# Two blocks on one core: row statistics in paused steps, a decay without mask matmuls, narrow time-step tiles, wider attention-value matmuls

## The chip, the cores and the metric

The program runs on one core of one Trainium2 chip. The metric is the device time of one execution in microseconds (us), the median over several runs. The kernel before takes 2222.25 us (three runs, 2221.23 to 2222.55). A difference below about 0.2%, 4.4 us, cannot be told from none here.

## What is computed

Two blocks follow each other on 512 rows of width 1024 (the second adds 16 meta rows: 528). All weight products are done to nearly float32 precision, each as three fp32r matmuls (high x high, high x low, low x high). The parts that the change touches:

```python
def ssd_chunked(x, dt, a_head, bm, cm):          # 32 heads, 4 groups, chunks of 128 rows
    a_cs = jnp.cumsum(a, axis=-1)                # a = dt * a_head, negative
    seg = a_cs[..., :, None] - a_cs[..., None, :]
    decay = jnp.where(causal, jnp.exp(jnp.where(causal, seg, 0.0)), 0.0)
    cb = jnp.einsum("bclgn,bcsgn->bcgls", cc, bc)
    y_diag = jnp.einsum("bcgrls,bcsgrp->bclgrp", cb[:, :, :, None] * decay, xs)
...
dt = jax.nn.softplus(dt_raw + dt_bias)           # dt_raw: 32 columns of h @ w_in
...
def layer_norm(x, g, b): ...                     # mean and variance over 1024
def rmsnorm(x, g): ...                           # mean square over 1024 or 512
...
o = jnp.einsum('bnhgqk,bnkhd->bnqhgd', p, v)     # sliding window, 8 heads of 64, 128 queries a block
```

## The kernel before

Activations are held transposed (features on partitions, rows on the free axis) as a high and a low tile. Weights stream from one DRAM array in the order in which they are used: `Weights.take` (line 99) hands out 128x128 blocks; units of eight blocks are loaded (`raw`), split on ScalarE (`whi`) and VectorE (`wlo`), and two of each are kept (`wheld` ones stay longer). `gemm` and `gemm_ab` issue three matmuls (`pm`) a block and segment; `gemm_ab` does the rows in two halves (`si` 0 and 1), all output tiles `m` of the first half, then those of the second, so that the second half's operand can still be in the making.

Work beside the gemms is written as generators. `start(gen, every)` (line 204) puts one into `tasks`; after each block `tick` (line 219) steps a task on every `every` ticks. `every=0` runs it to its end at once; `finish` (line 213) drains what is left. This sets only the order in which instructions are recorded; a list scheduler then orders each engine's queue by that order, by priorities (`tc.high_priority`) and by when it takes operands to be ready. On the chip each engine works its queue strictly in that order.

Row statistics need a sum over partitions. `colsum` (line 266) does it with `pcs` matmuls of one column, `meansq` scales on VectorE (`msv`), `rsqrt` (line 260) takes the power -1/2 on GpSimd (`rs_y`), `rstd_bcast` (line 284) spreads the result over partitions with `pbc` matmuls, and only then can VectorE scale the tiles. `pcs` and `pbc` are recorded directly one after the other, and pushed later by the priorities `LATE` and `LATE2` (40 and 60 places). `layer_norm`, `ssd_norm`, `pre_scale`, `post_pre` and `normed` all use it. In the text a place has the name of its use: sn0 to sn3 (state space groups), cn, ln1, ln2, ps (scale of the next block's input), an and yn (attention and convolution norms), post and post2 (after the mixer and the MLP); a last digit 0 or 1 is the half `si`, and ps has the layer ahead of it.

The state space part (`ssd_core`, line 595) makes for each of 32 heads a 128x512 tile `pA` = cumulated decay of the row, spread over partitions by a bf16 matmul with three-part decays, plus a mask matmul (`identb` x `mask_ssd`, -1e30 above the diagonal); four ScalarE Exp of 128 columns with bias `nacs` give `dec`, VectorE multiplies by `cbs`, and `py` matmuls use it. `time_steps` (line 506) makes dt with weights repeated four times, so that each of four 32-row strips of a 128x512 result holds all columns.

In `attention` (line 966) each unit (a block of 128 queries, two heads' pairs) multiplies the transposed probabilities `pT` with values `vt` (or `vm`, the 16 meta rows) into `po`, 64 output partitions a matmul, one head's 128 columns at a time.

Of the kernel before, what the change touches and what calls it, by code (L numbers as in the profile page):

```python
# [32 lines left out]
NV = 0  # L33
# [9 lines left out]
B_ID, B_SSD, B_ATT, B_SEL = 0, 128, 256, 512  # L43
NC16 = 512 + 32
# [71 lines left out]
def block_kernel(ctx, tc, xin, meta, wst, wdt, vec, c32, c16, out, order):  # L116
# [102 lines left out]
    def tick():  # L219
        for t in list(tasks):  # L220
            t[2] += 1
            while t[2] >= t[1]:
                t[2] -= t[1]
                if next(t[0], tasks) is tasks:
                    tasks.remove(t)
                    break
# [19 lines left out]
    identb = cb16[:, B_ID:B_ID + 128]  # L246
# [37 lines left out]
    def rstd_bcast(acc, tk, nt, width, eps):  # L284


        v = meansq(acc, tk, nt, width, eps)
        r = rsqrt(v, tk, nt)
        ps = PX("pbc")
        with tc.high_priority(offset=-LATE2):  # L290
            for j in range(nt):
                mmul(ps[:, j * tk:(j + 1) * tk], r[:, j:j + 1].to_broadcast([tk, 128]),
                     ident[:tk, :tk], start=True, stop=True)
        return ps[:, 0:nt * tk]
# [103 lines left out]
    def layer_norm(tiles, seg, cb, acc=None):  # L398

        c0, cn, tk, nt = seg  # L400
        sl = slice(c0, c0 + cn)
        if acc is None:
            acc = F("lnacc")[:, :cn]
            tt(acc, tiles[0][:, sl], tiles[1][:, sl], op=ALU.add)
            for i in range(2, 8):
                tt(acc, acc, tiles[i][:, sl], op=ALU.add)
                yield
        mu = PX("pmu")[:, :cn]
# [8 lines left out]
        r = rstd_bcast(sq.t, tk, nt, 1024, 1e-5)  # L417
# [88 lines left out]
    def time_steps():  # L506
        raw = A("wdt", F32).rearrange("p a b -> p (a b)")[:, 0:1024]
        dma(nc.scalar, raw, wdt)
        wh, wl = (A(f"wdt{j}").rearrange("p a b -> p (a b)")[:, 0:1024] for j in range(2))
        split((wh, wl), raw)  # L510
        ps = PM("pdt")
        for k in range(8):
            sl = slice(k * 128, (k + 1) * 128)
            mmul(ps, wh[:, sl], hA[k][:, 0, 0:512], start=(k == 0), stop=False)
            mmul(ps, wh[:, sl], hA[k][:, 1, 0:512], start=False, stop=False)
            mmul(ps, wl[:, sl], hA[k][:, 0, 0:512], start=False, stop=(k == 7))
# [4 lines left out]
        for c in range(4):  # L521
            q = slice(32 * c, 32 * c + 32)
            act(x[q], ps[q, c * 128:(c + 1) * 128], AF.Identity, bias=V("ssm_dt_bias")[q])
# [20 lines left out]
        dtT, nacs, dtds, cd = (tok[:, i] for i in range(4))  # L544
# [5 lines left out]
        ts(nacs, pv[:, 1], -1.0, None, op0=ALU.mult)  # L550
# [12 lines left out]
        mmul(pl[:, 0:128], ident[:, 127:128].to_broadcast([128, 128]), nacs.rearrange("p c h -> p (c h)"), start=True, stop=True)  # L563
        plv = pl[:, 0:128].rearrange("p (c h) -> p c h", c=4)
        act(cd, plv, AF.Exp, scale=-1.0)
        tt(dtds, nacs, plv, op=ALU.subtract)
        act(dtds, dtds, AF.Exp)
        tt(dtds, dtT, dtds, op=ALU.mult)
        DT["t"] = ahl, dtT, nacs, dtds, cd
# [25 lines left out]
    def ssd_core(gr):  # L595
        ahl, dtT, nacs, dtds, cd = DT["t"]
# [7 lines left out]
        acopy(cbs, pcb)  # L604
# [11 lines left out]
        for hf in range(2):  # L616
# [30 lines left out]
            for t in range(2):  # L647
# [64 lines left out]
    def ssd_norm(gr, acc, xs_):  # L712
        r = rstd_bcast(acc, 128, 4, 512, 1e-5)
# [10 lines left out]
    def conv_norm():  # L724
# [10 lines left out]
        yield from layer_norm([cts[i] for i in range(8)], (0, 512, 128, 4), cb)  # L735
# [109 lines left out]
    def ln1(si):  # L845
# [9 lines left out]
        yield from layer_norm([RS[i] for i in range(8)], x_seg(si), cb, RS["acc", si])  # L855
# [48 lines left out]
    def pre_scale(sq, si, seg, nxt):  # L904


        c0, cn, tk, nt = seg
        sq.flush()
        yield
        if nxt["square"]:  # L910
            v = meansq(sq.t, tk, nt, 1024, 1e-6)
            nxt["eps", si] = S([128, 4], "eps")[:tk, :nt]
            stt(nxt["eps", si], v, 1e-6, v, op0=ALU.mult, op1=ALU.mult)
        else:
            acopy(nxt["rb"][:, c0:c0 + cn], rstd_bcast(sq.t, tk, nt, 1024, 1e-6))

    def ln2(si):
# [11 lines left out]
        yield from layer_norm(h, (c0, cn, tk, nt), cb, RS["acc", si])  # L929
        scales.append(start(pre_scale(sq, si, seg, pre), EV['ps']))  # L930

    def post_pre(fs, sums, segs, si, gain, l, nxt, eps):
# [4 lines left out]
        r = rstd_bcast(sums[si].t, tk, nt, 1024, eps(si))  # L937
# [13 lines left out]
    def normed(ys, gain, l, seg, dst):  # L951
# [6 lines left out]
        r = rstd_bcast(sq.t, tk, nt, 512, 1e-6)  # L958
# [7 lines left out]
    def attention(l, Q, K, vt, vm, yP, norm, norms):  # L966
        def unit(b, pr):
# [58 lines left out]
            for i in range(2):  # L1026
                for j, (o, n, v) in enumerate(kbs):
                    for r in range(2):
                        mmul(po[64 * r:64 * r + 64, 128 * i:128 * i + nq], v[:n, 64 * r:64 * r + 64],
                             pTs[r][:n, (2 * j + i) * 128:(2 * j + i) * 128 + nq],  # L1030
                             start=(j == 0), stop=(j == len(kbs) - 1))
# [39 lines left out]
    for l in range(2):  # L1071
# [69 lines left out]
        for m in (0, 1, 2, 3)[WI - 2:]:  # L1141
            qkv[m] = qkv_tile(m)
            for p, (c0, cn) in zip(gemm(acts, w_in, one, m), one):
# [8 lines left out]
                              lambda si: normed(ya, "attn_out_g", l, psegs[si], yn[0:4]), norms), EV['att'])  # L1152
# [29 lines left out]
        def out_evac(m, si, ps):  # L1182
# [6 lines left out]
        post = lambda si: pend.append(start(post_pre(o, sums, psegs, si, "mix_post_g", l, pre, lambda si: 1e-6),  # L1189
                                            EV['post'] * (1 - si)))  # L1190
        gemm_ab(yn, w_out, range(8), gsegs, out_evac, lambda: post(0),
                first=(FO, 4, lambda: [run(normed(yc, "conv_out_g", l, psegs[si], yn[4:8]))
                                     for si in range(2)]))
# [47 lines left out]
        if l == 0:  # L1241
            ws.hold(16, WI)
        post = lambda si: pend.append(start(post_pre(f, fsums, psegs, si, "mlp_post_g", l, pre,
                                                     lambda si: mlp["eps", si]),
# [3 lines left out]
    while pend:  # L1248
# [10 lines left out]
SUML, LATE, LATE2 = 10, 40, 60  # L1259
# [5 lines left out]
      "ln1": 3, "ps": 4, "an": 4, "ln2": 0, "post": 5, "post2": 1.5}  # L1265

# [7 lines left out]
def _constants():  # L1274
# [15 lines left out]
    b[:, B_ID:B_ID + 128] = np.eye(128)  # L1290
    s = np.arange(128)
    m = np.where(s[:, None] <= s[None, :], 0.0, -1e30)
# [58 lines left out]
def _build():  # L1351
# [3 lines left out]
              ("wdt", (128, 1024), F32), ("vec", (128, NV), F32), ("c32", (128, NC32), F32),  # L1355
# [25 lines left out]
```

## Time and profile before

| | us |
|---|---|
| median of three runs | 2222.25 |
| the profiled execution, its own time | 2217.79 |
| its span | 2215.9 |
| TensorE busy | 2180.1 |
| VectorE busy | 1449.1 |
| ScalarE busy | 917.2 |
| GpSimd busy | 32.9 |

The page gives for each engine the time in which an instruction of its ran. A matmul's recorded duration overlaps the next one's: what a matmul costs in a stream is the distance from its start to the next start. "Idle before" is what an engine waited for before an instruction. The granted clock is TensorE's share of full speed in a stretch; it has two levels, 1.00 (2.4 GHz) and 0.50 (1.2 GHz).

### The profile page before, as it was taken

To read this page: it belongs to the slowest core of one execution; us is meant where nothing else is said; L and a number is where in the kernel's file an instruction comes from. 1 tells how busy PE (TensorE), PEld (TensorE's weight loads), DVE (VectorE), ACT (ScalarE), POOL (GpSimd) and SP (SyncE) were. 2 spreads that over 40 slices of the span, in tenths; PEclk is the share of its full clock that TensorE was granted. 3 is DMA by queue.
4 is the path that set the end of the run, shared out by engine and by line. 5 is a ranking of instruction groups with operands and counts; after the bars stand their busy time and mean duration, and the time that the engine had idled before them with its cause. 6 is when DMAs were issued, how large, how long until landed. Compare 5 with 4: busy or idle time off the path is not lost.

```text
span 2215.9 us, 33490 instructions
## 1 busy us (share of the span) xinstructions
PE 2180.1 (98%) x13786; PEld 1928.6 (87%) x13792; DVE 1449.1 (65%) x2650; ACT 917.2 (41%) x1700; POOL 32.9 (1%) x43
## 2 busy tenths in 40 slices
PE   8999999999999999999999999999999999999997
PEld 6887787878889888889999999999998899888897
DVE  7999899966668766636888653234378866423436
ACT  4344543444434444424646543224253554322323
POOL 0000000000000000000000000000000000000000
PEclk9999999999999999999999999999999999999999
DMA  4222121212232122224312212222251131222224
GB/s 154 96 81 73 58 82 71 96 59 94 95 133 77 58 95 95 95 96 172 125 58 96 77 40 95 96 90 83 96 182 58 60 131 39 96 95 95 95 96 152
DMA packets 32408, 206.86 MB, mean 93 GB/s; under 512 B 4608, under 2 KB 6912, under 8 KB 8192
## 3 DMA queue, kind: packets, MB, share of 16 engines
q1 hardware_dynamic: 30816, 203.01, 25.8%
q8 instruction: 108, 1.77, 0.3%
q10 hardware_dynamic: 1440, 1.71, 0.2%
q14 instruction: 44, 0.36, 0.1%
HBM read 202.61 MB, written 2.10 MB: 92 GB/s over the span
## 4 chain that ended last, share of the span: by engine, by line
PE 95%; DVE 1%; issue 1%; POOL 1%; DMA 0%; ACT 0%; POOLq 0%; DVEq 0%
PE pm L187 88%; PE po L187 2%; PE pbc L187 1%; PE py L187 1%; PE ppt L191 1%; POOL rs_y L263 1%; PE psc L187 1%; PE pA L187 1%; PE pcs L187 1%; PE pst L187 0%; PE ptx L191 0%; DMA raw<-wst 0%; DVE wlo L172 0%; PE pdt L187 0%; DVE bst L439 0%
## 5 line engine op out<-in xcount | busy, mean ns | idle before, releaser
L172 DVE TENSOR_TENSOR wlo<-raw,whi 128x1024 fp32r<-128x1024 f32 x335 | 409.8, 1224 | 499.9 <-ACT whi L184 498.1
L184 ACT CAST whi<-raw 128x1024 fp32r<-128x1024 f32 x335 | 351.1, 1049 | 755.3 <-PE pm L187 737.8
L187 PE MATMUL pm<-h,whi 128*128 128x512 f32 x1760 | 559.6, 397 | 0.0
L187 PE MATMUL pm<-r,whi 128*128 128x264 f32 (+2 forms) x2128 | 407.4, 302 | 0.0
L187 PEld LDWEIGHTS pm<-h,whi 128*128 128x128 f32 x1760 | 328.8, 188 | 77.0 <-issue 1.6
L187 PE MATMUL pm<-yn,whi 128*128 128x264 f32 (+2 forms) x1728 | 392.4, 330 | 0.1
L187 PE MATMUL pm<-h,wlo 128*128 128x512 f32 x880 | 349.4, 397 | 0.0
L187 PEld LDWEIGHTS pm<-r,whi 128*128 128x128 f32 x2128 | 318.5, 188 | 14.7 <-issue 0.2
L187 PEld LDWEIGHTS pm<-yn,whi 128*128 128x128 f32 x1728 | 275.6, 188 | 30.6 <-ACT yn L184 0.5
L187 PE MATMUL pm<-r,wlo 128*128 128x264 f32 (+2 forms) x1064 | 267.9, 301 | 0.1
L187 PE MATMUL pm<-yn,wlo 128*128 128x264 f32 (+2 forms) x864 | 247.2, 328 | 0.0
L187 PEld LDWEIGHTS pm<-h,wlo 128*128 128x128 f32 x880 | 165.0, 187 | 37.1 <-issue 0.9
L187 PE MATMUL pm<-ff,whi 128*128 128x264 f32 (+2 forms) x944 | 189.9, 307 | 0.0
L187 PEld LDWEIGHTS pm<-r,wlo 128*128 128x128 f32 x1064 | 178.9, 188 | 7.8 <-DVE wlo L172 0.3
L175 DVE SCALAR_TENSOR_TENSOR c<-v,vv,c 128x501 f32<-128x501 f32 (+27 forms) x240 | 167.0, 730 | 1.4 <-ACT c L181 0.9
L187 PEld LDWEIGHTS pm<-yn,wlo 128*128 128x128 f32 x864 | 147.3, 188 | 15.1
L187 PEld LDWEIGHTS pm<-ff,whi 128*128 128x128 f32 x944 | 146.4, 190 | 7.9
L187 PE MATMUL pm<-ff,wlo 128*128 128x264 f32 (+2 forms) x472 | 127.5, 306 | 0.0
L187 PE MATMUL pm<-yn,wheld 128*128 128x264 f32 (+1 forms) x960 | 125.8, 289 | 0.0
L187 PEld LDWEIGHTS pm<-yn,wheld 128*128 128x128 f32 x960 | 120.2, 192 | 0.6 <-issue 0.3
L187 PEld LDWEIGHTS pm<-ff,wlo 128*128 128x128 f32 x472 | 83.0, 190 | 4.0
L172 DVE TENSOR_TENSOR sum<-sum,sq 128x256 f32<-128x256 f32 (+2 forms) x171 | 73.2, 434 | 20.2 <-ACT sq L181 18.8
(255 smaller groups left out, 2372.9 us busy)
## 6 DMA issues: line engine op xcount, KB each, us to landing
raw<-wst SPq DMA_DIRECT2D x188, 1024.0 KB, 4.8
xr<-xin SPq DMA_DIRECT2D x4, 512.0 KB, 5.2
trig<-c SPq DMA_DIRECT2D x2, 528.0 KB, 5.7
raw<-wst SPq DMA_DIRECT2D x2, 512.0 KB, 7.5
out<-r ACTq DMA_DIRECT2D x8, 128.0 KB, 1.8
out<-r SPq DMA_DIRECT2D x8, 128.0 KB, 1.8
wdt<-wdt ACTq DMA_DIRECT2D x1, 512.0 KB, 5.3
vv<-vec SPq DMA_DIRECT2D x1, 385.0 KB, 7.8
```

The lines of the kernel that those rows point to most:

```text
L172: return first(nc.vector.tensor_tensor(o, a, b, op=op), o)
L175: return first(nc.vector.scalar_tensor_tensor(o, a, c, b, op0=op0, op1=op1), o)
L184: return first(nc.scalar.copy(o, a), o)
L187: r = first(nc.tensor.matmul(o, a, b, start=start, stop=stop), o)
L191: return first(nc.tensor.transpose(o, a, i), o)
L263: nc.gpsimd.tensor_tensor(y, v, mhalf[:p, :n], op=ALU.pow)
```

## The change

- Tasks count down to zero; a generator may yield a number, a pause of so many ticks (never less than `every`). `every=0` no longer runs a task to its end: it stops at the first pause. `colsum` and `rstd_bcast` lose their priorities; `rstd_bcast` pauses `GAP[use][0]` ticks ahead of `pcs` and `GAP[use][1]` ticks between `rs_y` and `pbc`. `finish` still drains without regard to pauses. The convolution's norms (yn) are started ahead of the output gemm.
- The 32 mask matmuls are gone. ScalarE computes `Relu(acs - pA)` (4 x 128 columns) and one more `Exp(-x)` over 512 columns; the mask (now 1 and 0) is multiplied into `cbs` once a group, on VectorE instead of a ScalarE copy.
- The time-step weights are 128x256 float32, not split and not repeated; 64 float32 matmuls of 32 output partitions x 128 columns, in four column positions, take the place of 24 fp32r matmuls of 128x512.
- `po`: where the block has 128 queries, both heads' 256 columns in one matmul (half as many).

```diff
     def start(gen, every=0):
         t = [gen, every, every / 2]
-        if every:
-            tasks.append(t)
-        else:
-            finish(t)
+        tasks.append(t)
+        if not every:
+            advance(t)
         return t
+    def advance(t):
+        while t[2] <= 0:
+            n = next(t[0], tasks)
+            if n is tasks:
+                tasks.remove(t)
+                break
+            t[2] += t[1] if n is None else max(n, t[1])
...
     def colsum(acc, tk, nt):
         ps = PX("pcs")
-        with tc.high_priority(offset=-LATE):
-            for j in range(nt):
-                mmul(ps[:tk, j:j + 1], acc[:, j * tk:(j + 1) * tk], ones[:, 0:1], start=True,
-                     stop=True)
+        for j in range(nt):
+            mmul(ps[:tk, j:j + 1], acc[:, j * tk:(j + 1) * tk], ones[:, 0:1], start=True, stop=True)
...
+        yield GAP[use][0]
         v = meansq(acc, tk, nt, width, eps)
         r = rsqrt(v, tk, nt)
+        yield GAP[use][1]
         ps = PX("pbc")
-        with tc.high_priority(offset=-LATE2):
-            for j in range(nt):
...
-        ps = PM("pdt")
+        ps = PM("pdt")[:, 0:128]
         for k in range(8):
...
+            sl = slice(k * 32, (k + 1) * 32)
+            for j in range(2):
+                for c in range(4):
+                    mmul(ps[32 * c:32 * c + 32], raw[:, sl],
+                         hA[k][:, j, c * 128:(c + 1) * 128].bitcast(F32),
+                         start=(k == 0 and j == 0), stop=(k == 7 and j == 1))
...
-        acopy(cbs, pcb)
+        tt(v3(cbs), v3(pcb), mask_ssd, op=ALU.mult)
...
                     mmul(pA, sel[:, h + r:h + r + 1].to_broadcast([128, 128]), ahl, start=True,
-                         stop=False)
-                    mmul(pA, identb, mask_ssd, start=False, stop=True)
+                         stop=True)
...
-                        act(dec[:, sl], pA[:, sl], AF.Exp, bias=nacs[:, c, h + r:h + r + 1])
+                        act(dec[:, sl], pA[:, sl], AF.Relu, scale=-1.0, bias=acs[:, c, h + r:h + r + 1])
+                    act(dec, dec, AF.Exp, scale=-1.0)
...
-            for i in range(2):
+            for i in range(1 if nq == 128 else 2):
+                cn = 256 if nq == 128 else nq
...
-                        mmul(po[64 * r:64 * r + 64, 128 * i:128 * i + nq], v[:n, 64 * r:64 * r + 64],
+                        c = (2 * j + i) * 128
+                        mmul(po[64 * r:64 * r + 64, 128 * i:128 * i + cn], v[:n, 64 * r:64 * r + 64],
...
+GAP = {"cn": (1, 3), "sn0": (1, 3), "sn1": (1, 3), "sn2": (1, 3), "sn3": (1, 3), "ln10": (2, 20), "ln11": (2, 41),
+       "ln20": (2, 36), "ln21": (2, 40), "ps00": (2, 26), "ps01": (2, 20), "ps10": (2, 20), "ps11": (2, 20), "an0": (2, 3), "an1": (2, 20), "yn0": (2, 6), "yn1": (2, 6),
+       "post0": (2, 6), "post1": (2, 12), "post20": (2, 12), "post21": (2, 28)}
```

How the change moves TensorE's queue, at three places. First a head of the state space part, before and then now (`pA` the decay tile, `cb` the mask and selector constants, `pm` the gemm that runs beside it):

```order
L187 MATMUL pm<-h_114,wlo 128x512
L187 LDWEIGHTS cb_92
L187 MATMUL pA<-ahl,cb_92 128x512
L187 LDWEIGHTS cb_92
L187 MATMUL pA<-cb_92 128x512
```

```order
L187 MATMUL pm<-h_114,wlo 128x512
L187 LDWEIGHTS cb_92
L187 MATMUL pA<-ahl,cb_92 128x512
L187 MATMUL pm<-h_115,whi 128x512 x2
```

The second `pA` matmul, the mask, is gone; the gemm follows at once.

Second, TensorE where the second block's first projection changes from half 0 to half 1 (place ln21; `ff22` to `ff29` are its eight operand tiles), before and then now:

```order
L187 MATMUL pbc_8652<-cc_91,rs_y_8650 128x128 x2
L187 MATMUL pm_8846<-ff25_6108,wheld_8788 128x264
L187 MATMUL pm_8846<-ff25_6108,wheld_8789 128x264
L187 MATMUL pm_8846<-ff26_6183,wheld_8788 128x264 x2
L187 MATMUL pm_8846<-ff26_6183,wheld_8789 128x264
L187 MATMUL pm_8846<-ff27_6258,wheld_8788 128x264 x2
L187 MATMUL pm_8846<-ff27_6258,wheld_8789 128x264
L187 MATMUL pm_8846<-ff28_6333,wheld_8788 128x264 x2
L187 MATMUL pm_8846<-ff28_6333,wheld_8789 128x264
L187 MATMUL pm_8846<-ff29_6408,wheld_8788 128x264 x2
L187 MATMUL pm_8846<-ff29_6408,wheld_8789 128x264
L187 MATMUL pm_8873<-ff22_5907,wheld_8576 128x264
```

```order
L187 MATMUL pm_8809<-ff28_6366,wheld_8751 128x264 x2
L187 MATMUL pm_8809<-ff28_6366,wheld_8752 128x264
L187 MATMUL pm_8809<-ff29_6441,wheld_8751 128x264 x2
L187 MATMUL pm_8809<-ff29_6441,wheld_8752 128x264
L187 MATMUL pbc_8836<-cc_91,rs_y_8702 128x128 x2
L187 MATMUL pm_8892<-ff22_5940,wheld_8609 128x264
L187 MATMUL pm_8918<-ff22_5940,wheld_8613 128x264
L187 MATMUL pm_8977<-ff22_5940,wheld_8648 128x264
```

Before, 14 gemm matmuls of half 0 stand between `pbc` and the first matmul of half 1 (the row `pm_8873<-ff22`); now none does.

Third, TensorE after the first layer's MLP (place post21; `r2_16` to `r2_23` are the next layer's operand tiles), before and then now:

```order
L187 MATMUL pcs_15118<-cc_91,sum_14994 88x1 x3
L187 MATMUL pm_15383<-r2_21_13589,wheld_15278 128x264
L187 MATMUL pm_15383<-r2_21_13589,wheld_15279 128x264
L187 MATMUL pm_15383<-r2_22_13654,wheld_15278 128x264 x2
L187 MATMUL pm_15383<-r2_22_13654,wheld_15279 128x264
L187 MATMUL pm_15383<-r2_23_13721,wheld_15278 128x264 x2
L187 MATMUL pm_15383<-r2_23_13721,wheld_15279 128x264
L187 MATMUL pm_15426<-r2_16_13258,wheld_15282 128x264 x2
L187 MATMUL pbc_15126<-cc_91,rs_y_15124 128x88 x3
```

```order
L187 MATMUL pcs_15188<-cc_91,sum_15043 88x1 x3
L187 MATMUL pm_15389<-r2_16_13259,wheld_15319 128x264 x2
L187 MATMUL pm_15389<-r2_16_13259,wheld_15320 128x264
L187 MATMUL pm_15389<-r2_17_13326,wheld_15319 128x264
L187 MATMUL pbc_15285<-cc_91,rs_y_15194 128x88 x3
```

Between `pcs` and `pbc` stood ten gemm matmuls, and now stand four.

## Rows read from the trace of the kernel before

**Rows 1.** The page: busy time, share of the span, instructions.

```profile
PE 2180.1 (98%) x13786; PEld 1928.6 (87%) x13792; DVE 1449.1 (65%) x2650; ACT 917.2 (41%) x1700; POOL 32.9 (1%) x43
```

**Rows 2.** Waits of TensorE: us in total, times, longest us.

```profile
PE pbc L187 <- POOL rs_y L263: 13.9, 16, 1.6
...
PE pm L187 <- ACT ff L181: 0.3, 1, 0.3
```

**Rows 3.** Chain of waits, 165 to 177 us: start, us, what.

```profile
165.51 0.45 PE pA L187 x2
165.96 4.17 PE pm L187 x18
170.12 1.02 PE py L187 x16
```

**Rows 4.** Chain of waits, whole span.

```profile
45.55 5.59 PE pdt L187 x24
...
1147.17 1.47 PE po L187 x16
...
1167.12 1.02 PE po L187 x16
```

**Rows 5.** Groups by shape: count | busy us, mean ns of one | idle before.

```profile
L181 ACT ACTIVATE dec<-pA,tok 128x128 f32<-128x128 f32 x128 | 37.2, 372 | 34.8 <-PE pA L187 33.3 <-PE py L187 1.5
L172 DVE TENSOR_TENSOR dec<-dec,cbs 128x512 f32<-128x512 f32 x32 | 21.9, 687 | 3.9 <-ACT dec L181 3.8
L181 ACT ACTIVATE fth<-cg 128x512 f32<-128x512 f32 x22 | 13.9, 632 | 46.3 <-DVE cg L175 46.3
```

**Rows 6.** GpSimd's powers: all (ns min/median/max), then six in time, us.

```profile
L263 POOL TENSOR_TENSOR rs_y<-msv,mhalf x29: 695/847/2104, 230.4 to 2205.9; 128x2 f32<-128x2 f32 x12, 88x3 f32<-88x3 f32 x12, 128x4 f32<-128x4 f32 x5
...
311.68 1.43 POOL L263 TENSOR_TENSOR rs_y<-msv,mhalf 128x4 f32<-128x4 f32 x1 [79.86 <-DVE msv L178]
...
518.30 1.01 POOL L263 TENSOR_TENSOR rs_y<-msv,mhalf 128x4 f32<-128x4 f32 x1 [108.82 <-DVE msv L178]
...
1045.10 1.61 POOL L263 TENSOR_TENSOR rs_y<-msv,mhalf 128x2 f32<-128x2 f32 x1 [336.43 <-DVE msv L178]
1067.92 1.80 POOL L263 TENSOR_TENSOR rs_y<-msv,mhalf 88x3 f32<-88x3 f32 x1 [21.21 <-DVE msv L178]
...
1218.49 0.97 POOL L263 TENSOR_TENSOR rs_y<-msv,mhalf 88x3 f32<-88x3 f32 x1 [32.01 <-DVE msv L178]
1223.98 1.05 POOL L263 TENSOR_TENSOR rs_y<-msv,mhalf 88x3 f32<-88x3 f32 x1 [4.52 <-DVE msv L178]
```

**Rows 7.** Timeline of TensorE at 1044 us (place ln20).

```profile
1044.15 0.61 PE L187 MATMUL pcs<-cc,sum 128*128 128x1 f32 x4
...
1046.76 0.71 PE L187 MATMUL pbc<-cc,rs_y 128*128 128x128 f32 x4 [1.44 <-POOL rs_y L263]
```

**Rows 8.** Timeline of TensorE at 1223 us (place yn).

```profile
1223.08 0.56 PE L187 MATMUL pcs<-cc,sum 128*88 128x1 f32 x6
1225.09 0.54 PE L187 MATMUL pbc<-cc,rs_y 88*128 88x88 f32 x2 [1.45 <-POOL rs_y L263]
```

**Rows 9.** Chain of waits, 1080 to 1092 us (place ln21).

```profile
1079.92 3.29 PE pm L187 x27
...
1085.48 0.43 DVE r L172
...
1085.93 1.09 ACT r L181 x2
1087.03 0.41 ACT ff L181
```

**Rows 10.** Stretches: us, PE, PEld, DVE, ACT, POOL busy, granted clock, DMA share, GB/s.

```profile
1047.80:1051.20 3.40, 3.40 (x19) 3.40 (x18) 2.12 (x7) 2.13 (x4) 0.00 (x0) 0.50 0.67 275
...
1225.30:1232.10 6.80, 6.55 (x32) 6.32 (x32) 4.86 (x13) 3.16 (x8) 0.85 (x1) 0.50 0.01 4
...
1802.10:1805.60 3.50, 3.38 (x16) 3.39 (x17) 3.50 (x11) 2.50 (x6) 0.06 (x1) 0.51 0.02 5
```

More of the change, by code (lines that the diff above doesn't have):

```diff
@@ L220, in tick @@
         for t in list(tasks):
[L221 to L226, printed above, removed]
+            t[2] -= 1
+            advance(t)
     cc = const.tile([128, C_COS], F32, tag="cc", name="cc")
@@ L396, in block_kernel, with layer_norm @@
     ALL = [(0, 512)]
-    def layer_norm(tiles, seg, cb, acc=None):
+    def layer_norm(tiles, seg, cb, use, acc=None):
         c0, cn, tk, nt = seg
@@ L407, in layer_norm @@
                 yield
+        yield GAP[use][0]
         mu = PX("pmu")[:, :cn]
@@ L416, in layer_norm @@
         sq.flush()
-        r = rstd_bcast(sq.t, tk, nt, 1024, 1e-5)
+        r = yield from rstd_bcast(sq.t, tk, nt, 1024, 1e-5, use)
         for i in range(8):
@@ L520, in time_steps @@
         x, e, u, s = w("dtx"), w("dte"), w("dtu"), w("dts")
[L521 to L523 removed]
+        act(x, ps, AF.Identity, bias=V("ssm_dt_bias"))
         stt(e, x, -1.0, x, op0=ALU.mult, op1=ALU.max)
@@ L543, in time_steps @@
         tok = const.tile([128, 4, 4, 32], F32, tag="tok", name="tok")
-        dtT, nacs, dtds, cd = (tok[:, i] for i in range(4))
+        dtT, acs, dtds, cd = (tok[:, i] for i in range(4))
         pt = PX("pdt2")
@@ L595, in ssd_core @@
     def ssd_core(gr):
-        ahl, dtT, nacs, dtds, cd = DT["t"]
+        ahl, dtT, acs, dtds, cd = DT["t"]
         bc, xs_ = XG[gr]
@@ L733, in cb @@
             del cts[i]
-        yield from layer_norm([cts[i] for i in range(8)], (0, 512, 128, 4), cb)
+        yield from layer_norm([cts[i] for i in range(8)], (0, 512, 128, 4), cb, "cn")
     gate = {}
@@ L853, in cb @@
             tt(lo, x, hi.bitcast(F32), op=ALU.subtract)
-        yield from layer_norm([RS[i] for i in range(8)], x_seg(si), cb, RS["acc", si])
+        yield from layer_norm([RS[i] for i in range(8)], x_seg(si), cb, f"ln1{si}", RS["acc", si])
     ws.hold(8, 6)
@@ L910, in pre_scale @@
         if nxt["square"]:
+            yield GAP["ps00"][0]
             v = meansq(sq.t, tk, nt, 1024, 1e-6)
@@ L914, in pre_scale @@
         else:
-            acopy(nxt["rb"][:, c0:c0 + cn], rstd_bcast(sq.t, tk, nt, 1024, 1e-6))
+            r = yield from rstd_bcast(sq.t, tk, nt, 1024, 1e-6, f"ps{nxt['layer']}{si}")
+            acopy(nxt["rb"][:, c0:c0 + cn], r)
     def ln2(si):
@@ L927, in cb, with post_pre @@
             pre_tile(i, pre, sl, sq)
-        yield from layer_norm(h, (c0, cn, tk, nt), cb, RS["acc", si])
+        yield from layer_norm(h, (c0, cn, tk, nt), cb, f"ln2{si}", RS["acc", si])
         scales.append(start(pre_scale(sq, si, seg, pre), EV['ps']))
-    def post_pre(fs, sums, segs, si, gain, l, nxt, eps):
+    def post_pre(fs, sums, segs, si, gain, l, nxt, eps, use):
         c0, cn, tk, nt = segs[si]
@@ L936, in post_pre @@
         sums[si].flush()
-        r = rstd_bcast(sums[si].t, tk, nt, 1024, eps(si))
+        r = yield from rstd_bcast(sums[si].t, tk, nt, 1024, eps(si), f"{use}{si}")
         sq = Sum(cn, SUML)
@@ L957, in normed @@
         sq.flush()
-        r = rstd_bcast(sq.t, tk, nt, 512, 1e-6)
+        r = yield from rstd_bcast(sq.t, tk, nt, 512, 1e-6, use)
         for i in range(4):
@@ L1188, in block_kernel @@
         ws.hold(8, UP)
-        post = lambda si: pend.append(start(post_pre(o, sums, psegs, si, "mix_post_g", l, pre, lambda si: 1e-6),
+        post = lambda si: pend.append(start(post_pre(o, sums, psegs, si, "mix_post_g", l, pre, lambda si: 1e-6, "post"),
                                             EV['post'] * (1 - si)))
+        cnorms = [start(normed(yc, "conv_out_g", l, psegs[si], yn[4:8], f"yn{si}")) for si in range(2)]
         gemm_ab(yn, w_out, range(8), gsegs, out_evac, lambda: post(0),
-                first=(FO, 4, lambda: [run(normed(yc, "conv_out_g", l, psegs[si], yn[4:8]))
-                                     for si in range(2)]))
+                first=(FO, 4, lambda: [finish(t) for t in cnorms]))
         post(1)
```

51 lines of the change are left out of this document (22 added, 29 removed).

## The prediction

> **What bounds the kernel now.** I read the page's busy times first. TensorE is busy in 98% of the span and no other engine in more than 65% [rows 1], so the time falls only where TensorE gets less work, waits less, or runs at a higher clock. Next I read TensorE's own waits: GpSimd's power ends 16 of them, 13.9 us together [rows 2], and they are the largest item that a different order could remove. Third, the chain of waits prices the three kinds of matmul that the change touches [rows 3, 4]. Last, the stretches show where the clock fell to half: three times behind such waits, while TensorE had work [rows 10]. About 0.2%, 4.4 us, is what a measurement can tell from no change.
>
> **The change part by part.** The sum is made against the profiled execution's own 2217.8 us, which lies 4.5 us under the median of the runs (2222.25); I subtract the same from both.
>
> *Mask matmuls.* A pair, decay and mask, takes 0.45 us [rows 3], half of it the mask's: 32 x 0.22 = **7.0 us less**. Nothing lies beside them on TensorE, so all of it counts. In exchange ScalarE does a pass of 512 columns more a head; the nearest row is the Tanh of that size, 0.63 us [rows 5], so 32 x 0.63 = 20 us of ScalarE. ScalarE is at 41% [rows 1], so this costs only where TensorE reaches `py` too early. From `pA` to `py` lie four short passes (37.2 us for 128, 0.29 each, 1.2 together [rows 5]), the new 0.63, and VectorE's multiply, 0.69 [rows 5]; with the hand-overs 2.7 us, or 12 gemm matmuls at 0.23 (18 in 4.17 [rows 3]). In the new order 27 of the 32 heads have 12 or more between; five have 8 to 10 and wait some 0.1 to 0.3 us, as far as other small matmuls there don't cover it. I take **0.5 us more**; the bounds are 0 and five times 0.7. The mask's product on VectorE, four times, and the ScalarE copy that it replaces touch no wait of TensorE in rows 2 and cost nothing; if VectorE ran late there, `py` would wait for 0.1 us a group.
>
> *Time steps.* 24 matmuls of 512 columns take 5.6 us now [rows 4]. The new 64 are plain float32, and each is two instructions, as with `py` (eight matmuls, 16 records [rows 3]). `py` has the same 128 columns in two column positions and takes 1.02/16 = 0.064 us an instruction. No row shows four positions. If four work only as two do, 128 x 0.064 = 8.2 us; if they work abreast, half, 4.1; if one after the other, twice, 16.3. I take 4.1, since two tiles of 64 columns and four of 32 fill the array alike: **1.5 us less**, with the ends 1.5 less and 10.7 more. The missing split of these weights (one pass each of ScalarE and VectorE) frees engines that nothing waits for here.
>
> The Trainium skill, page TensorE: Matmul & The Clock Gate, Part 3, says that a weight load overlaps a running matmul only where its row group differs. All four column positions use the same rows, so by that rule each of the 128 loads would stand in the open and the part would come out near the upper end. The 16 `py` instructions, also on the same rows, take 0.064 us each with their loads [rows 3], which speaks against it; I follow the row.
>
> *Attention values.* A unit takes 1.02 us for 16 instructions [rows 4]: half as many, each twice as long, give nothing. Four units (the first block of 128 queries, two pairs in two layers) take 1.47 [rows 4], because they go from 16 meta rows to 128 and back twice; now once. Two changes' worth of the excess 0.45 goes: 4 x 0.3 = **1.2 us less**, between 0 and 1.8.
>
> *Pauses.* The power takes 0.70 to 2.10 us, 0.85 at the median [rows 6]. How long TensorE stands depends on how many gemm matmuls the order puts between `pcs` and `pbc`. At ln20 there are four (0.12 us each: 27 in 3.29 [rows 9]), the power takes 1.61 and TensorE idles 1.44 [rows 6, 7]; so idle is the power less 0.17, and 0.12 less for each further one. At yn none stands between: 1.05 and 1.45 [rows 6, 8], the power plus 0.40. With this I go through the new order.
>
> - Cleared: ln10 (4 to 22), ln11 (4 to 12), ln20 (4 to 19), both post1 (4 to 21 and 20), post20 (8 to 23), ps10 (14 to 27), the first yn norm of each layer (0 to over 30 and 12).
> - Not cleared, as `finish` drains the task before the pause is over or the sums come late: ps00 (4 to 7; power 1.80) 1.27; ps01 and ps11 (4; 0.85) 0.68 each; post21 (10 to 4; the longest power, 2.10) 1.93; the second yn norm of each layer (0, but the first one's `pbc` stand between) 0.65 each.
> - New: sn1 (9 to 5 at 0.23 us; power 1.43) 1.43 + 0.40 - 1.15 = 0.68; sn3 (11 to 3; 1.01) 0.70; an1 of layer 0 (12 to 5; 0.97) 0.68 [rows 6].
> - New of another kind: at ln21 `pbc` now stands behind the last matmul of half 0, and nothing is left to do until the first tile of half 1 has passed VectorE (0.43) and ScalarE (1.09 and 0.41): 1.93 us [rows 9]. Before, 14 matmuls covered all of it but 0.3 [rows 2].
>
> Together 9.9 us. Before it was 13.9 + 0.3 [rows 2] less the kernel's last `pbc`, which doesn't change (0.70 + 0.40): 13.1. So **3.2 us less**. `pcs` itself waits no longer than it did.
>
> *Clock.* In the three stretches at half clock TensorE ran gemm matmuls for about 3.4, 2.9 and 2.1 us (the parts behind the waits at ln20 and at both yn [rows 10]); half of that, 4.2 us, was lost. All three waits shrink. But post21 and ln21 now idle 1.9 us each, longer than the 1.44 at ln20 that a low stretch followed. I let one stretch of 3.4 us come back, 1.7 lost: **2.5 us less**, between 0 and 4.2.
>
> Sum: -7.0 + 0.5 - 1.5 - 1.2 - 3.2 - 2.5 = -14.9. The profiled execution should take 2202.9 us, the median **2207**.
>
> **The rivals.**
> *All waits go.* If the pauses do what they are written for also at the places that I count as uncleared, 13.1 us of waits and 4.2 of the clock go: -7.0 + 0.5 - 1.5 - 1.2 - 13.1 - 4.2 = -26.5, or 2196. For it: seven places are cleared by the order alone. Against it: post21, ps01, ps11 and ln21 stand in the queue with four or no matmuls to cover them. Chance 0.12.
> *The column tiles run in turn.* Then the time-step part takes 16.3 us instead of 4.1, and the result is 2207 + 12.2 = 2219, no difference that can be told. It is also what the skill's rule on weight loads above would make of it, and `py`'s row speaks against it. Chance 0.09.
> *The decay becomes ScalarE's.* ScalarE works in order, and the casts `whi` for the gemm stand in the same queue. If the longer pass delays either `dec` or the next weights by its full 0.63 us in each head, TensorE loses 20.2 us instead of 0.5: 2207 + 19.7 = 2227, slower. It decides as soon as fewer than 12 gemm matmuls stand between `pA` and `py`, or `whi` has no time to spare. Against it: 27 of 32 heads have the distance, and TensorE waited for no `dec` and no `whi` before [rows 2]. Chance 0.04.
> That the mask matmuls stay, or the pauses move nothing, is excluded by the order.
>
> **How the numbers follow.** Forecast 0.75, the rivals 0.12, 0.09 and 0.04. The forecast's own range takes the time steps at 8.2 instead of 4.1 (+4.1), the clock at 0 (+2.5) and new waits at `py` (+2) on one side, and half of the uncleared waits gone (-5) and all of the clock (-1.7) on the other: 2200 to 2215. With the first rival, 2196 to 2215 holds 0.8 or a little more. The first two cases are faster by over 0.2%; of the forecast I give 0.02 to the margin. Faster 0.85, within 0.2% 0.11, slower 0.04.
>
> **What would show it.** Right: no `pA<-cb` without `ahl`; the time-step matmuls near 4 us in the chain; TensorE's waits for `rs_y` near 9 us in all, with post21 the longest and ln10, ln20 and post1 gone; an idle of about 2 us before `pm` at ln21, ended by ScalarE; at most one or two stretches at half clock. Wrong: waits of `py` for `dec` or of gemm matmuls for `whi` between 150 and 490 us (third rival); time steps over 8 us (second); a sum of `rs_y` waits under 3 us (first) or over 13.

## The result, and the profile after

The changed kernel takes 2197.68 us (median of four runs, 2197.28 to 2198.88), the kernel before 2221.74: 24.1 us less, a ratio of 0.9899 (95% interval 0.9887 to 0.9910). The forecast was 2207 in a range of 2196 to 2215, and faster. The direction is right and the forecast saw 14.9 us of the gain. The time lies in the range, but below 2200, where the forecast's own range ended; the part down to 2196 stood there for the first rival, whose mechanism did not come about. That it lies inside the range is to that extent luck. The profiled executions are 20.5 us apart (2217.79 and 2197.28), their spans 20.6. Why the medians are further apart is told under the clock.

The page, busy time by engine, answers to [rows 1]: TensorE is still busy in 98% of the span, 18.5 us less in all; ScalarE is busy 13.6 us more.

```profile
PE 2161.6 (98%) x13731; PEld 1912.5 (87%) x13736; DVE 1449.8 (66%) x2653; ACT 930.8 (42%) x1724; POOL 30.7 (1%) x43
```

TensorE's waits (us in total, times, longest), to be read against [rows 2]:

```profile
PE pbc L187 <- POOL rs_y L266: 6.7, 11, 1.1
PE pm L187 <- ACT ff L181: 2.0, 1, 2.0
PE pcs L187 <- DVE sum L172: 1.7, 2, 1.5
PE pm L187 <- ACT wheld L184: 1.2, 2, 0.9
PE pm L187 <- DVE wheld L172: 1.1, 2, 0.5
PE ppt L191 <- DVE p L178: 0.7, 1, 0.7
PE pm L187 <- DVE r L175: 0.5, 1, 0.5
...
PE pdt L191 <- DVE dtx L175: 0.3, 1, 0.3
```

The wait for the power has halved, from 13.9 to 6.7 us, but seven kinds of wait stand beside it where two stood before. Leaving out the start of the program, all waits together fell only from 16.0 to 14.2 us: most of what the pauses cleared came back elsewhere. No row is a wait of `py`, nor of a gemm matmul for `whi`.

The time steps, in TensorE's timeline, and a head's decay matmul and the attention values, in the chain of waits, answer to [rows 3] and [rows 4]; the ScalarE passes, by shape, to [rows 5].

```profile
45.69 3.70 PE L187 MATMUL pdt<-h,wdt 128*32 128x128 f32 x128
```

```profile
164.28 0.23 PE pA L187
...
1135.36 1.16 PE po L187 x8
```

```profile
L181 ACT ACTIVATE dec<-pA,tok 128x128 f32<-128x128 f32 x128 | 37.5, 370 | 18.9 <-PE pA L187 16.4 <-PE po L187 1.7 <-PE pE L187 0.4
L181 ACT ACTIVATE dec<-dec 128x512 f32<-128x512 f32 x32 | 20.4, 637 | 0.6
```

The 128 time-step instructions take 3.63 us up to the next matmul's start (5.59 before). A head's decay takes 0.23 where decay and mask took 0.45. The first block's attention-value unit takes 1.16 (1.47 before). The new Exp pass takes 0.64 a head, as the Tanh row said.

Place ln21, chain of waits and TensorE's timeline, answers to [rows 9]:

```profile
1074.05 0.43 DVE r L172
...
1074.51 1.09 ACT r L181 x2
1075.60 0.41 ACT ff L181
```

```profile
1073.37 0.65 PE L187 MATMUL pbc<-cc,rs_y 128*128 128x128 f32 x4
1076.06 0.88 PE L187 MATMUL pm<-ff,wheld 128*128 128x264 f32 x5 [2.04 <-ACT ff L181]
```

The same three pieces, now in the open: 2.04 us, where 1.93 was forecast.

Stretches answer to [rows 10] (us, then busy time of PE, PEld, DVE, ACT, POOL, granted clock, DMA share, GB/s):

```profile
1075.90:1079.30 3.40, 3.24 (x26) 3.24 (x27) 2.97 (x9) 3.40 (x10) 0.00 (x0) 1.00 0.10 41
1215.30:1218.70 3.40, 3.40 (x18) 3.40 (x17) 3.18 (x5) 1.55 (x3) 0.00 (x0) 0.51 0.44 120
```

Of 13.6 us at half clock within the work, 3.4 are left, at layer 0's yn. In the stretch behind ln21's wait, the longest of all, the clock stayed at full speed.

The ledger, by the prediction's own terms (profiled executions, us):

| term | forecast | measured | read from |
|---|---|---|---|
| mask matmuls and new waits at `py` | -6.5 | -6.7 | x1_decay, 500th to 2000th gemm matmul |
| time steps | -1.5 | -2.0, and +0.5 | 5.59 to 3.63; a new wait at the transposition of dt (0.3 in the list, 0.5 from start to start) |
| attention values | -1.2 | -1.2 | four units, 1.47 to 1.16 |
| waits | -3.2 | -2.1 | TensorE's list, without the program's start and dt |
| clock | -2.5 | -5.1 | below |
| not foreseen | 0 | -4.0 | the rest of 20.6 |

The clock's line: in each half-clock stretch I summed by how much the distances between matmuls' starts exceed those of the same matmuls at full clock. A stretch of 3.4 us costs 1.5. Before, the three cost 6.6; now the one costs 1.5. Both figures are those of one execution.

### The profile page after: what moved, and what is told of

Its sections match the earlier page's. It is cut to its first block, busy times and chain, and to the rows that moved or that the text cites. A ratio compares the mean times of both kernels' runs of the same rounds, so it can differ in the third digit from the quotient of the medians.

```text
span 2195.3 us, 33380 instructions
## 1 busy us (share of the span) xinstructions
PE 2161.6 (98%) x13731; PEld 1912.5 (87%) x13736; DVE 1449.8 (66%) x2653; ACT 930.8 (42%) x1724; POOL 30.7 (1%) x43
## 4 chain that ended last, share of the span: by engine, by line
PE 93%; DVE 4%; issue 1%; DMA 1%; ACT 1%; POOL 0%; POOLq 0%; DVEq 0%; ACTq 0%
PE pm L187 86%; PE po L187 1%; PE py L187 1%; PE pbc L187 1%; PE ppt L191 1%; PE pcs L187 1%; DVE c L175 1%; PE psc L187 1%; DVE wlo L172 1%; DMA raw<-wst 1%; PE pst L187 0%; POOL rs_y L266 0%; DVE qkv L172 0%; PE ptx L191 0%; DVE r L172 0%
## 5 line engine op out<-in xcount | busy, mean ns | idle before, releaser
L175 DVE SCALAR_TENSOR_TENSOR c<-v,vv,c 128x511 f32<-128x511 f32 (+27 forms) x240 | 168.3, 731 | 1.5 <-ACT c L181 0.9
```

The lines of the kernel that those rows point to most:

```text
L175: return first(nc.vector.scalar_tensor_tensor(o, a, c, b, op0=op0, op1=op1), o)
```

## The experiments

The kernel before ran beside each group of runs; its medians were 2220.1 to 2221.4, and its one run beside x12_form took 2217.2.

### One part at a time

Each kernel is the one before with one part of the change's diff: x1_decay the decay, x2_pauses the pauses, x3_dt_av time steps and attention values.

> The kernel before with the decay part alone (no mask matmuls, Relu and one more Exp on ScalarE, mask in cbs). By the prediction's terms: 7.0 us less for the mask matmuls and 0.5 more for waits at py, 6.5 us less in all, about 2215 us beside 2221.7. If py never waits: 7.0 less. If the changed kernel's gain of 7.3 us between the 250th and the 2000th gemm matmul comes from this part alone, although two new waits of 0.7 us (sn1, sn3) stand there, the part is worth 8 to 9 us. If the longer ScalarE pass delayed each head (third rival), 13 us more.

Measured: 2213.32 us (2212.15 to 2214.39), ratio 0.9966 (0.9954 to 0.9979): 7.1 less. In the trace the 1500 gemm matmuls of the state space part take 6.7 us less, 1.7 in each of the four groups of heads. TensorE's list shows no wait for `dec`.

> The kernel before with the pauses alone (GAP, tasks that stop at a pause, no priorities, yn norms started ahead). By the prediction's terms: waits 3.2 us less and clock 2.5 less, 5.7 in all, about 2216 us. If the parts add up and the others are worth what their matmuls show in the changed kernel's trace (mask 6.9, time steps 1.9, attention values 1.2), the pauses are worth the rest of the measured 20.6 us of span: 10.6, about 2211. Then TensorE's waits for rs_y should again stand near 6.7 us, with one stretch at half clock instead of three. If the parts work on each other, more or less than that.

Measured: 2207.11 us (2206.44 to 2212.06), ratio 0.9943 (0.9928 to 0.9958): 13.3 less, more than twice the forecast's 5.7. The largest of TensorE's waits in its profile:

```profile
PE pbc L187 <- POOL rs_y L267: 6.9, 11, 1.1
PE pm L187 <- ACT wheld L184: 2.3, 2, 1.4
PE pm L187 <- ACT ff L181: 2.0, 1, 2.0
PE pcs L187 <- DVE sum L172: 1.5, 1, 1.5
```

All waits fell by 0.9 us only. There is no half-clock stretch inside the work, so 6.6 us of clock came back. Of the 11.1 us of span that the part is worth, 3.6 are neither.

> The kernel before with the time steps and the attention values alone. By the prediction's terms 1.5 + 1.2 = 2.7 us less, about 2219 us; by the changed kernel's trace 1.9 + 1.2 = 3.1 us. If the shorter attention values also help where other matmuls are recorded between them (before, four of the sixteen units are cut in two or more pieces by pbc or gemm matmuls, and a cut unit takes up to 1.9 us instead of 1.0), up to 1.5 us more.

Measured: 2216.64 us (2214.27 to 2217.46), ratio 0.9981 (0.9971 to 0.9990): 3.8 less, more than the 2.7 and the 3.1 of the parts alone and within the 1.5 more that fewer cut units could give. The three parts sum to 24.2 us; the whole is 24.1. They add up, as far as intervals of 2 to 3 us on each can tell.

### The column tiles, one after the other

```diff
-        for k in range(8):
-            sl = slice(k * 32, (k + 1) * 32)
-            for j in range(2):
-                for c in range(4):
+        for c in range(4):
+            for k in range(8):
+                sl = slice(k * 32, (k + 1) * 32)
+                for j in range(2):
```

> The changed kernel with the loop over the four column positions outermost, so that neighbouring time-step matmuls stand in the same position; the same 64 matmuls, 128 instructions. If the time steps are short (3.65 us) because neighbours in different positions work abreast, each of the 128 now costs what a lone float32 instruction of 128 columns costs in the trace (0.109 us, transposes and pbc): 14.0 us, so 10.3 us more, about 2208. If the position makes no difference and an instruction with 32 output columns is short of itself, it stays at 3.65 us and 2197.7. If only the weight load in the same rows counted, both orders would cost the same too, since all positions use the same rows.

Measured: 2208.00 us (2206.85 to 2208.85), as the first theory says (it put the time steps at 14.0 us). Its chain of waits:

```profile
46.41 12.87 PE pdt L187 x128
```

The same 128 instructions take 12.87 us instead of 3.63, 0.10 each: neighbours in four different positions work abreast, and the second rival needs no more than an unlucky loop order. By the Trainium skill's rule of the prediction (TensorE: Matmul & The Clock Gate, Part 3: a weight load overlaps only where its row group differs) both orders should cost alike, since all positions use the same rows; these two traces do not bear it out for column positions.

### A longer ScalarE chain

```diff
                         act(dec[:, sl], pA[:, sl], AF.Relu, scale=-1.0, bias=acs[:, c, h + r:h + r + 1])
+                    act(dec, dec, AF.Copy)
                     act(dec, dec, AF.Exp, scale=-1.0)
```

> The changed kernel with one more pass of 512 columns on ScalarE in each of the 32 heads (a copy of dec onto itself ahead of the Exp). From pA to py then lie 2.7 + 0.63 = 3.3 us, 14 to 15 gemm matmuls. In this order, which the compiler's scheduler has drawn apart again, the smallest distances are 12, 12, 13, 13 and then 16. If the longer ScalarE chain costs only where py comes too early: four heads wait 0.3 to 0.6 us each, 1 to 2 us in all, and TensorE's waits show py for dec there. If ScalarE's time itself were on the path (third rival's mechanism): 32 x 0.63 = 20 us more. If the scheduler's estimate holds: no wait at py, no change.

Measured: one run, 2200.11 us, 2.4 above the median of the changed kernel; of that 1.5 is a half-clock stretch behind ln21. ScalarE's passes over `dec` and TensorE's `py`, by shape:

```profile
L181 ACT ACTIVATE dec<-dec 128x512 f32<-128x512 f32 x64 | 40.7, 636 | 1.2
L187 PE MATMUL py<-dec,xt 128*64 128x128 f32 x256 | 20.9, 281 | 0.0
```

ScalarE did 20 us more, and `py` did not wait once. The third rival has no ground even at twice the pass: the scheduler moves `py` away as `dec` grows longer (least distances of 12 gemm matmuls in x8_exp2's order, of 8 to 10 in the changed kernel's). My distance of 12 matmuls was too strict; the new waits that I put at 0.5 us are zero.

### Priorities put back beside the pauses

```diff
+        with tc.high_priority(offset=-LATE):
             for j in range(nt):
                 mmul(ps[:tk, j:j + 1], acc[:, j * tk:(j + 1) * tk], ones[:, 0:1], start=True, stop=True)
...
+        with tc.high_priority(offset=-LATE2):
             for j in range(nt):
```

> The changed kernel with the two priorities (40 and 60 places) put back around pcs and pbc, pauses kept: both mechanisms at once. In the order pcs and pbc are cut into pieces again and stand later; gemm matmuls between the last pcs and the first pbc: sn3 13 (3 before), ps00 11 (7), ps01 15 (4), an1 of layer 0 8 (3 to 5), post21 7 (4). By the idle rule 2.7 us of waits go there; at yn of layer 0 pbc now stands behind all 72 matmuls of the first four tiles' half, which costs up to 2 us more. If only waits count: 1 us less, about 2197. If it costs by itself to cut small groups and scatter them among gemm matmuls (the pauses alone took 11.1 us of span away, of which the trace shows 6.6 at half clock and 0.9 of idle time, so some 4 are left for that): 3 us more, about 2201.

Measured: 2214.54 us (2213.94 to 2216.83), ratio 0.9972 (0.9961 to 0.9983): both expectations missed by far. The spans differ by 19.5 us. Four half-clock stretches instead of one cost 6.8 more, and all waits together 5.6 more, these three above all:

```profile
PE pm L187 <- ACT wheld L184: 5.8, 2, 3.3
PE pbc L187 <- POOL rs_y L266: 5.5, 9, 1.2
PE pm L187 <- ACT h L181: 2.3, 2, 1.1
```

The power's wait did shrink, as the distances said. But a later `pbc` makes everything behind it later: VectorE scales the tiles later, and the gemm matmuls that use them wait instead (`h` at ln1, the split tiles of yn, which the list puts down to `wheld`). Some 7 us are neither clock nor wait. They go with the number of times that TensorE's queue changes from one kind of matmul (told by the tile that it writes) to another: 534 before, 426 with the pauses alone, 421 in the changed kernel, 544 here. A part has a price in the traces. Outside the half-clock stretches, the first gemm matmul behind a group of `pcs` or `pbc` takes 0.08 us longer to the next start than one behind another gemm matmul. There are 83 such places before, 53 with the pauses alone, 53 in the changed kernel and 85 here: 2.6 of the 7 us, and 2.4 of the 3.6 us of x2_pauses.

### What such a change costs

```diff
                             mmul(py[64 * r:64 * r + 64, sl], xt[:, c, hc:hc + 64], decs[r][:, sl],
                                  start=True, stop=True)
+                        if c == 1:
+                            w = 64 if t else 128
+                            mmul(py[0:w, 256:257], ident[:, 0:w], ones[:, 0:1], start=True, stop=True)
```

By form is meant here how much of the array a matmul uses: a full-width one writes 128 output partitions, a `py` matmul 64, in one of two column positions.

> The changed kernel with one more small float32 matmul of a single column in the middle of each of the 16 py units (written to a column that is overwritten afterwards, the result stays): 128 output partitions wide in the units with t = 0, 64 wide, as py itself is, in those with t = 1. Uncut units take 0.92 to 1.02 us now; the matmul's own two instructions some 0.1 to 0.2 (pcs: four in 0.36). If it costs to change between matmuls that use the whole array and matmuls in two column positions (a py pair that stands alone among gemm matmuls takes 0.36 us, in a unit 0.13): units with t = 0 take 0.2 to 0.25 us more than units with t = 1, about 1.4 against 1.2. If a cut costs nothing by itself, both take the same, about 1.1 to 1.2.

Measured: one run, 2198.36 us. Units of 16 instructions took 0.92 us and now take 1.39 with the 128-wide insert, 0.98 with the 64-wide one; units of 14 took 1.02 and take 1.48 and 1.02. TensorE's timeline of one of the first kind:

```profile
168.65 0.66 PE L187 MATMUL py<-dec,xt 128*64 128x128 f32 x8
169.24 0.38 PE L187 MATMUL py<-cc 128*128 128x1 f32 x2
169.55 0.66 PE L187 MATMUL py<-dec,xt 128*64 128x128 f32 x8
```

A full-width matmul inside a two-position unit costs 0.46 us, a matmul of the unit's own form at most 0.06. Some of the 0.46 can be the full-width matmul's own: its two instructions take 0.14 to 0.22 us among others of their form (`pcs` at sn0 in the kernel before). So 0.25 to 0.4 us is the way there and back between forms, and x12_form showed the first of the two cases expected, only more strongly. The Trainium skill (TensorEngine Tiling (Array Packing), Key Properties) says that changing the tiling mode drains the engine; the runs agree. Counted by form (rows and columns used, each rounded up to 32, 64 or 128), the changes in TensorE's queue are 175 before, 155 with the pauses alone, 151 in the changed kernel and 170 in x7_prio. By an estimate from the 0.25 to 0.4 us, 20 changes fewer, ten ways there and back, are worth 2.5 to 4 us. With the 2.4 us behind `pcs` and `pbc` that is more than the 3.6 us of x2_pauses, so the two do not simply add. In the kernel before, this timeline shows one of its attention-value units:

```profile
1186.73 0.65 PE L187 MATMUL po<-pT,vt 128*64 128x128 f32 x6
1187.31 0.45 PE L187 MATMUL pbc<-cc,rs_y 88*128 88x88 f32 x2
1187.69 0.43 PE L187 MATMUL po<-pT,vt 128*64 128x128 f32 x2
1188.05 0.45 PE L187 MATMUL pbc<-cc,rs_y 88*128 88x88 f32 x2
1188.44 0.43 PE L187 MATMUL po<-pT,vt 128*64 128x128 f32 x2
```

The priorities had spread `pbc` piece by piece between them; from start to start the unit's own pieces took 1.89 us, and in the changed kernel it takes 1.01 in one piece. With a second such unit (1.53 to 1.01) that is 1.4 of the 4.0 us that I had not foreseen. Another 1.1 went at sn0, where `pbc` and single gemm matmuls had cut `pst`, `po` and `py`. For the remaining 1.5 no place was settled.

### Shorter and longer pauses

x9_ln2: `GAP` of ln20 and ln21 (2, 20). x10_sn7: `"sn": 7` in `EV`. x11_ps01: both `"sn": 7` and a priority of -60 for `pbc` at ps01.

> The changed kernel with shorter pauses at ln20 and ln21 (20 ticks each, so that ln20's pbc stands 4 gemm matmuls behind pcs as before, not 19, and ln21's pbc stands 20 matmuls ahead of half 1, not 0). If the wait only moved from ln20 to ln21 (VectorE starts on ln21's chain as late as ln20's pbc lets it): 1.4 us of wait come back at ln20, up to 1 us at ps00, and the 2.0 us before the first matmul of half 1 go: 0.6 us less to 0.7 more, plus or minus one half-clock stretch (1.5 us). If the pause at ln20 was free and ln21's wait has a cause of its own: 1.4 us or more are added and the 2.0 us stay.

Measured: 2202.72 us (2200.09 to 2204.78), 5.0 more than the changed kernel; the expectation of about no change missed. The wait before half 1 did go. But `pbc` waits again at all three places:

```profile
1038.60 0.72 PE L187 MATMUL pbc<-cc,rs_y 128*128 128x128 f32 x4 [1.43 <-POOL rs_y L266]
...
1061.62 0.56 PE L187 MATMUL pbc<-cc,rs_y 88*128 88x88 f32 x3 [1.62 <-POOL rs_y L266]
...
1078.77 0.71 PE L187 MATMUL pbc<-cc,rs_y 128*128 128x128 f32 x4 [1.29 <-POOL rs_y L266]
```

ln20's wait came back whole (1.43 us, as in the kernel before). At ps00 the power takes 1.80 again instead of 0.96, and at ln21 1.61 instead of 0.70. Two half-clock stretches followed, at ln20 and at ps00. So ln20's pause pays, although it makes ln21 later; half of my trade was there, but I had kept the powers fixed.

> The changed kernel with the ssd norms stepped every 7 ticks instead of every 10. A pause is never shorter than the task's step, so sn's pause of 3 ticks is one of 10, and sn1 and sn3 are drained before it ends. With 7, fifteen gemm matmuls of 0.23 us stand between pcs and pbc at both: the waits of 0.7 us each go, 1.4 us less, about 2196.3, and pbc waits for rs_y 5.3 us in all. If the earlier norm work delays VectorE in the state space part instead: no change or up to 1 us more.

Measured: 2197.93 us (2196.38 to 2198.90). Both waits are gone, the list has 5.7 us for `rs_y`, and still the time is the changed kernel's. Its stretches:

```profile
1076.00:1079.40 3.40, 3.40 (x18) 3.40 (x17) 3.05 (x8) 3.40 (x9) 0.00 (x0) 0.50 0.02 5
1216.00:1219.40 3.40, 3.40 (x18) 3.40 (x17) 3.33 (x5) 1.69 (x4) 0.00 (x0) 0.50 0.44 113
```

The first is the one that the changed kernel's profile had at full clock: 1.4 us won and 1.5 lost behind ln21, whose wait of 2.0 us is the same in both.

> The changed kernel with the ssd norms every 7 ticks (both waits of 0.7 us go, as in x10_sn7's trace) and pbc at ps01 alone moved back by a priority of 60 places (15 gemm matmuls behind pcs instead of 4; its wait of 0.8 us goes). 2.2 us less than the changed kernel, about 2195.5, if the half-clock stretch behind ln21, which x10_sn7 showed and the changed kernel's profile didn't, comes in about as many executions as in the changed kernel; 1.5 us more where it comes in every one. What else moves back with pbc at ps01 would show as waits of pm or psc behind 1100 us.

Measured: 2198.61 us (2195.83 to 2200.41), ratio to the kernel before 0.9900 (0.9884 to 0.9917). Its list has 5.2 us for `rs_y`, near the 5.0 that are left of x10_sn7's 5.7 without ps01's wait. Its profile has the stretch behind ln21 and none at yn. No version found here is measurably faster than the changed kernel.

### What lengthens the power

```diff
         r = rsqrt(v, tk, nt)
+        for _ in range(3):
+            nc.vector.scalar_tensor_tensor(acc[:tk], acc[:tk], v[:, 0:1], acc[:tk], op0=ALU.mult, op1=ALU.add)
         yield GAP[use][1]
```

> The changed kernel with three more VectorE operations behind each msv (multiply-add of the sum tile, which is no longer needed, with msv as scalar: operands in SBUF alone, 256 to 512 columns); they change no result. In the changed kernel GpSimd's power takes 0.70 (two columns), 0.85 (three) or 1.01 us (four) alone and longer where an SBUF-only VectorE operation starts just before it. Theory A (it waits for the remainder of the VectorE operation that runs when it starts): where one of the new operations directly follows msv, the power takes its base plus some 0.3 us at 256 columns and 0.5 at 512, however many follow. Theory B (it waits until VectorE leaves SBUF): base plus 0.9 to 1.8 where all three follow each other. Theory C (the data decide): no change at any place.

> The same three operations, but one operand of each is read from PSUM (a pcs column, spread over the row); the sum tile that they overwrite is no longer needed. Theories A and B with the remark that operations which read PSUM did not lengthen the power in the changed kernel: base (0.70, 0.85 or 1.01 us) wherever such an operation directly follows msv. If any VectorE operation lengthens it: the same times as with operands in SBUF alone.

Measured: one run each, 2209.14 and 2214.07 us; the added operations delay much else, so only the powers are read. None of the three theories holds as written. At ln20, VectorE's and GpSimd's timelines of the changed kernel and then of x5_vsbuf:

```profile
1036.04 1.22 DVE L172 TENSOR_TENSOR wlo<-raw,whi 128x1024 fp32r<-128x1024 f32 x1
1036.20 1.61 POOL L266 TENSOR_TENSOR rs_y<-msv,mhalf 128x2 f32<-128x2 f32 x1 [336.38 <-DVE msv L178]
```

```profile
1036.50 0.51 DVE L292 SCALAR_TENSOR_TENSOR sum<-sum,msv 128x256 f32<-128x256 f32 x1
1036.94 1.21 DVE L172 TENSOR_TENSOR wlo<-raw,whi 128x1024 fp32r<-128x1024 f32 x1
1036.55 0.69 POOL L266 TENSOR_TENSOR rs_y<-msv,mhalf 128x2 f32<-128x2 f32 x1 [336.22 <-DVE msv L178]
```

The new operation needs `msv` and so starts with the power (0.05 us ahead by the rows), and `wlo` comes after: the power fell from 1.61 to 0.69. What counts is an operation with both tensors in SBUF (the memory of the tiles; PSUM is the one that matmuls write) that has run for more than 0.05 us when the power starts. The power then takes 0.70, 0.85 or 1.01 us (two, three or four columns) and what is left of that operation less 0.14. This gives 387 of the 406 powers of all 14 profiles to within 0.025 us.

x6_vpsum alone does not tell PSUM from SBUF, since most of its operations start with the power, as those of x5_vsbuf do. But 52 of the 406 powers started beside an operation with a PSUM operand that had run for longer, and none of them was lengthened. One is at ln21 in the changed kernel:

```profile
1072.39 0.42 DVE L172 TENSOR_TENSOR qkv<-pm,rb 128x264 f32<-128x264 f32 x1
1072.56 0.69 POOL L266 TENSOR_TENSOR rs_y<-msv,mhalf 128x2 f32<-128x2 f32 x1 [15.35 <-DVE msv L178]
```

Of the 19 powers that the rule misses, 11 are off by less than 0.04 us. Among the others is the longest one of the kernel before, at post21:

```profile
1653.72 0.42 DVE L172 TENSOR_TENSOR sum<-sum,sq 128x264 f32<-128x264 f32 x1
1654.06 1.21 DVE L172 TENSOR_TENSOR wheld<-raw,wheld 128x1024 fp32r<-128x1024 f32 x1
1653.88 2.10 POOL L263 TENSOR_TENSOR rs_y<-msv,mhalf 88x3 f32<-88x3 f32 x1 [24.53 <-DVE msv L178]
```

From what is left of `sum` the rule gives 0.97. The 2.10 come out if the power also waits for the second operation, `wheld`: 0.85 and its end less 0.14. The same stands in x1_decay and x3_dt_av, and a like case in x7_prio at 1065 us. At ps00 in the changed kernel `r` is followed by `wheld` just so, and the power took 0.96, the value for `r` alone. Why it waits for a second operation at some places stays open; for these four, theory B is nearer.

## Why the prediction was right, and where it was wrong

**Right, by its steps.** The mask term, the attention term and the time steps came out at their sizes, the latter two by the mechanism given (fewer changes between 16 rows and 128; four positions abreast). These two were read from the units' times; only the four positions were tested by themselves (x4_turn). The order's reading held: ln10, ln20, post1, post20 and ps10 are cleared, sn1 and sn3 wait anew, and ln21 shows its two microseconds. The idle rule held where its inputs did: post21 has four matmuls, a power of 0.85 and 0.66 us of idle (the rule gives 0.68). At sn1, sn3 and the second yn norms it came out 0.1 to 0.2 us too high.

**Mis-sized: the clock**, "2.5 us less, between 0 and 4.2". It measured 5.1, beyond its own bound. Two things failed. I counted the gemm matmuls only (4.2 us lost before), where the trace lost 6.6: they ran 3.4, 3.2 and 2.5 us at half clock, not 3.4, 2.9 and 2.1, and `pcs` and `pbc` ran at half clock as well. And I let waits of 1.9 us at post21 and ln21 keep the clock low; post21's wait was 0.66, and ln21's was followed by a half-clock stretch in four profiles with the same wait (x4_turn, x8_exp2, x10_sn7, x11_ps01), in a fifth the clock fell during it (x7_prio), and in three it did not fall (the changed kernel, x2_pauses, x12_form). The medians go with the clock too. In 33 executions of the kernel before that ran beside the experiments, those with a mean granted clock of 0.996 took 2217.2 us on average, with 0.995 2218.6, with 0.994 2220.3, with 0.993 2221.9. The profiled execution was one at 0.995, the median lies between 0.993 and 0.994, and the changed kernel has 0.997 or 0.998. By these averages about 2.5 of the 3.6 us by which the medians differ more than the profiles go with the clock, and the sum against a profile that lies 4.5 us under the median should have carried that.

**Mis-sized: the waits**, "9.9 us" after the change. The power's waits came to 6.7 instead of 9.0, because powers were taken over from the trace of before. The 2.10 us of post21 and the 1.80 of ps00 belonged to VectorE operations that no longer stood there (0.85 and 0.96 now); an1 of layer 1, which I had at nothing, rose to 1.07. Against that, 3.8 us came that no step named: yn's later tiles (2.3), `ppt` for `p`, a gemm matmul for `r`, and dt's transposition. The two errors offset each other in part only: the waits fell by 2.1 us (dt's left out), not by 3.2.

**Not seen at all:** that the priorities cost by themselves, by cutting small units. This is the 4.0 us of the ledger that no term held; 2.5 of it were found at cut units, for the rest the cause is not shown. The prediction priced only idle time behind `pcs` and `pbc`, and looked at their distance, never at what stood between them.

The first rival gave the nearest time (2196), for a wrong reason: 14.2 us of waits are still there. The second was excluded by 3.63 us for the time steps, the third by the absence of any wait at `py`.

## What to carry to other kernels

On an engine that is busy 98% of the time, a reordering is worth its waits, the half-clock stretches behind them, and the changes of matmul form that it makes or saves; here the last two gave more than the first. Issue matmuls of one form together, and neighbours in different column positions next to each other. Where a duration taken from a trace is long against its own kind (a power of 2.10 us beside 0.85), find out what ran beside it before carrying it to a new order.

## What was not expected of the hardware

A GpSimd operation on three columns takes 0.85 us, or up to 2.10, depending on what VectorE runs when it starts. The Trainium skill (SBUF — State Buffer, SBUF: two separate sides) says that the two share a pair of ports, locked by whichever starts first, against VectorE operations with two SBUF inputs. The lengthening by an operation that is already running, and its absence with a PSUM operand, agree. That the later one is blocked for the whole instruction is not seen the other way round: at ln20 in x5_vsbuf `wlo` starts while the power runs and takes 1.21 us, as it does elsewhere.

The same wait of 2.0 us at the same place was followed by half clock in some profiles and not in others, so a gain of 1.4 us (x10_sn7) can vanish in it. So it is with the waits at layer 0's yn (0.93 to 0.95 and 0.54 us in all these profiles): half clock followed in the changed kernel, x4_turn, x8_exp2 and x10_sn7, and not in x2_pauses, x9_ln2, x11_ps01 and x12_form. What decides it was not tried.
